# One decoder layer on Trainium2: where copies, additions and weight differences stand among seven block products

## The chip, the cores and the metric

The kernel runs on 1 core of one Trainium2 chip, in fp32 stored data and fp32r matrix products. The metric is the device time of one execution in microseconds (us): median of several executions, smaller is better.

## The reference, cut to what matters

One layer of a decoder with 512 tokens and a model width of 1024. A mixer (retention and dilated attention, gated) gives a 512 x 1024 matrix that is multiplied by `w_o` and added to the residual `x`. Then comes an MLP with 4096 hidden columns, and a gated embedding at the end.

```python
x = x + (gate_r * ret_branch + gate_a * att_branch) @ w_o      # 512x1024 @ 1024x1024
u = rmsnorm(x, g_mlp) @ w_up                                   # 1024 -> 4096
x = x + jnp.square(jax.nn.relu(u)) @ w_down                    # 4096 -> 1024
gate_p = jax.nn.sigmoid(rmsnorm(x, g_ple) @ w_ple_gate)
return x + gate_p * (p_i @ w_ple_proj)
```

The change touches the product with `w_o` and the four products that `w_down` is cut into (each 512 x 1024 by 1024 x 1024). These are the five places where the kernel calls `seven_gemm`.

## The kernel before, in words

**Precision.** Each fp32 factor is split into two parts: hi (rounded to fp32r, by ScalarE, L237) and lo (the difference to the original, by VectorE, L238). A product is three matmuls: hi*hi, hi*lo, lo*hi (`mm3`, L249 to L251), all with 512 columns, into one PSUM bank of 128 x 512.

**Seven products.** `seven_gemm` computes a 2 x 2 block product with seven block products instead of eight. Its left factors (sums and differences of the activation blocks) are prepared by `seven_left`. A product is called here by the number `m` that the code gives it; they run in the order 4, 3, 5 (interleaved), 2, 1, 7, 6. Each has two halves `u` of the contraction and two halves `p` of 128 tokens: 6 matmuls for each pair (u, p), 24 in all. The results lie in PSUM banks: products 4 and 2 share the bank pair named 4 (product 2 accumulates onto 4), 3 and 6 share pair 3, 5 and 7 share pair 5, and product 1 has a pair of its own, `banks[1, p]`. Pairs 3 and 4 show in the trace as `pg`, pairs 5 and 1 as `pb`.

**What is done with a full bank.** ScalarE copies bank pair 4 to the tiles `m4` (L1040, it is needed again after product 1). `acc` (L1026, VectorE) adds a bank with a factor to the residual tiles `x`. When a half of a token tile of `x` is final, `done` calls `ready`, where one is given, which queues a transposition for a few ticks later: `split_T` transposes the 128 x 512 piece on TensorE into a bank (L325), and the result is read twice, hi by ScalarE (L338) and lo by VectorE (L339): `h2h`, `h2l` in the first call, `h3h`, `h3l` in the last. For the tiles that are final after product 5, **the bank that takes the transposes is `banks[1, p]`**, the one into which product 1 is computed next (`free` in `ready`). The three calls between have no `ready` and no transposes.

**Weights.** `plan_seven` lists 14 weight units for each call, numbered 0 to 13 here (n to n + 13 in the code): 0 to 5 for products 4, 3, 5 of both halves, 6 and 7 for product 2, 8 and 9 for product 1, 10 and 11 for product 7, 12 and 13 for product 6. Units 0, 1, 3, 4 and 10 to 13 are sums: one load by SyncE's queue (L200), a second load that adds to it by GpSimd's queue (L202). Units 8 and 9 have no load: they are unit 6 minus unit 2 and unit 7 minus unit 5, subtracted in place by VectorE (L215). `ahead` loads and splits units in order up to `used + n` where `units(n)` adds the class's `AHEAD`: with AHEAD = 3, product number k in order of units splits up to unit k + 3 before its matmuls. There are 6 raw buffers and 4 pairs of split buffers (`whi`, `wlo`), so that the split of a unit waits for the product four units before it.

**Order.** In the first call (with `w_o`) and in the last (last quarter of `w_down`), ScalarE and VectorE execute their instructions strictly in the order of the program text (`manual_schedule`); in the three calls between, and on all other engines and queues, a list scheduler orders the instructions by program order and modelled readiness. In `tail`, AHEAD is 3 when the first and the last call begin; `seven_gemm` sets it to 2 ahead of product 7, so it is 2 when the calls between begin. In `tail`, one tick pops one queued function; a tick comes after each half `p` of a product.

Of the kernel before, what the change touches and what calls it, by code (L numbers as in the profile page):

```python
# [13 lines left out]
AF = mybir.ActivationFunctionType  # L14
ALU = mybir.AluOpType
# [57 lines left out]
def R(ap):  # L73
    return ap.bitcast(F32R)


class Block:
# [86 lines left out]
    def plan_seven(self, w, r0):  # L164


        q = lambda i, j, u: w[r0 + 512 * i + 256 * u : r0 + 512 * i + 256 * (u + 1), 512 * j : 512 * (j + 1)]
        n = len(self.plan)
        for u in range(2):
            self.plan.append(((q(1, 0, u), q(0, 0, u)), None))  # L170
            self.plan.append(((q(0, 1, u), q(1, 1, u)), None))
            self.plan.append((q(1, 1, u), None))
        for u in range(2):
            self.plan.append((q(0, 0, u), None))
        self.differences[n + 7] = [(n + 6 + u, n + 2 + 3 * u) for u in range(2)]
        for u in range(2):
            self.plan.append(((None, n + 6 + u, n + 2 + 3 * u), None))
        for u in range(2):
            self.plan.append(((q(1, 0, u), q(1, 1, u)), None))
        for u in range(2):  # L180
            self.plan.append(((q(0, 0, u), q(0, 1, u)), None))
# [23 lines left out]
    def ahead(self, n):  # L205
        while len(self.loaded) < min(len(self.plan), self.used + n):
            i = len(self.loaded)
            self.fetch(i + 1)
            raw, g0 = self.raws[i]
            src = self.plan[i][0]  # L210
            if isinstance(src, tuple) and src[0] is None:
                g0 = None
            self.loaded.append(self.split_unit(raw, g0))
            for v, w in self.differences.get(i, ()):
                self.nc.vector.tensor_tensor(self.raws[v][0], self.raws[v][0], self.raws[w][0], op=ALU.subtract)  # L215

    def units(self, n):
        self.ahead(n + (0 if self.pinned else self.AHEAD))
# [782 lines left out]
    def seven_gemm(self, U, xs, f, ready):  # L1001


        nc = self.nc
        LEFT = {1: 3, 2: 4, 3: 0, 4: 6, 5: 1, 6: 5, 7: 2}
        banks = {}

        def product(m, bank, u, first, last):
            (wh, wl), = self.units(1)
            for p in range(2):  # L1010
                if first and m != 1:
                    banks[bank, p] = self.gbank() if m in (3, 4) else self.bank("pb")
                ps = banks[bank, p]
                for k in range(2):
                    kk = 2 * u + k
                    c = slice(LEFT[m] * 256 + p * P, LEFT[m] * 256 + (p + 1) * P)
                    sh, sl = (R(U[i][kk].rearrange("p a b -> p (a b)")[:, c]) for i in range(2))
                    self.mm3(ps, sh, sl, wh[:, k], wl[:, k], first and k == 0, last and k == 1, m != bank)
                self.tick()

        X = lambda i, j, p: xs[2 * i + p][:, 512 * j : 512 * (j + 1)]

        def acc(i, j, p, v, sign=0):
            t, x = 2 * i + p, X(i, j, p)
            c = sign * NT + t
            nc.vector.scalar_tensor_tensor(x, v, f[:, c : c + 1], x, op0=ALU.mult, op1=ALU.add)  # L1026

        def done(i, j, p):
            if ready is not None:
                ready(2 * i + p, j, banks.get((1, p)))  # L1030

        for u in range(2):
            for m in (4, 3, 5):
                product(m, m, u, u == 0, u == 1)
        m4 = []
        for p in range(2):
            banks[1, p] = self.bank("pb")
        for p in range(2):
            t = self.tmp("m4")
            nc.scalar.activation(t, banks[4, p], AF.Copy)  # L1040
            m4.append(t)
            acc(0, 1, p, banks[3, p])
            acc(0, 1, p, banks[5, p], 1)
            done(0, 1, p)
        for u in range(2):
            product(2, 4, u, False, u == 1)
        for p in range(2):
            acc(1, 0, p, banks[4, p])
            done(1, 0, p)
            acc(1, 1, p, banks[4, p], 1)  # L1050
        for u in range(2):
            product(1, 1, u, u == 0, u == 1)
        for p in range(2):
            nc.vector.tensor_tensor(m4[p], m4[p], banks[1, p], op=ALU.add)
            acc(0, 0, p, m4[p])
            acc(1, 1, p, m4[p])
        self.AHEAD = 2
        for u in range(2):
            product(7, 5, u, False, u == 1)
        for p in range(2):  # L1060
            acc(0, 0, p, banks[5, p])
            done(0, 0, p)
        for u in range(2):
            product(6, 3, u, False, u == 1)
        for p in range(2):
            acc(1, 1, p, banks[3, p])
            done(1, 1, p)
# [165 lines left out]
```

## Time and profile before

| | us |
|---|---|
| median of 3 runs (993.36 to 993.88) | 993.45 |
| the profiled execution | 993.55 |
| its span, first to last instruction | 991.8 |
| TensorE matmul busy in it | 984.9 |
| VectorE busy | 648.8 |
| ScalarE busy | 462.1 |
| first call of `seven_gemm` on TensorE | 558.15 to about 599.9 |
| last call | 900.15 to about 941.6 |

How to read it: the span is that of the profiled execution; its time also holds some 1.75 us around the span. In rows of the timeline the first number is the start in us from the start of the span, the second the duration, then engine, line, operation, tiles as output<-inputs, and in brackets the idle time of the engine before the row with what ended it. PE is TensorE, DVE VectorE, ACT ScalarE, POOL GpSimd, SPq the queue of SyncE. A matmul is listed with its duration from entry to end, and the next one enters before it ends.

### The profile page before, as it was taken

The numbers are of one execution on the slowest core, as the hardware profiler recorded it, in microseconds if no ns is written. First come the engines' busy times: TensorE is split into PE (matmuls) and PEld (weight loads), VectorE is DVE, ScalarE is ACT, GpSimd is POOL, SyncE is SP. The second block draws the span as 40 slices with busy tenths as digits, with TensorE's granted clock in tenths as the row PEclk, the third lists the DMA queues.
The fourth block names the chain that finished last, engine by engine and source line by source line (L and its number), as shares of the span: only waits on it lengthen the run. The fifth ranks groups of instructions, "written<-read, shape, count | busy, mean of one in ns | idle before, by whom it ended". The sixth has DMA issues, their size and how long they took to land.

```text
span 991.8 us, 12456 instructions
## 1 busy us (share of the span) xinstructions
PE 984.9 (99%) x4588; PEld 826.7 (83%) x4588; DVE 648.8 (65%) x1015; ACT 462.1 (47%) x939; POOL 98.1 (10%) x98
## 2 busy tenths in 40 slices
PE   9999999999999999999999999999999999999998
PEld 6888899889888888888888888888888888888886
DVE  7858675774869345454733796678667769767953
ACT  6635344433334334243423448664563565465451
POOL 0310120220000010001002000100101001000000
PEclk9999999999999999999999999999999999999999
DMA  9723122333234322222446486758749767875911
GB/s 333 262 85 87 44 85 85 113 98 98 83 109 153 124 63 76 96 65 86 162 135 156 137 218 201 185 141 221 184 132 226 187 159 170 228 174 128 298 54 54
DMA packets 90910, 141.16 MB, mean 142 GB/s; under 512 B 6320, under 2 KB 40672, under 8 KB 90848
## 3 DMA queue, kind: packets, MB, share of 16 engines
q1 hardware_dynamic: 79824, 119.36, 37.3%
q0 software_dynamic: 10880, 20.97, 12.6%
q8 instruction: 36, 0.59, 0.2%
q14 instruction: 26, 0.21, 0.1%
q10 hardware_dynamic: 144, 0.02, 0.0%
HBM read 136.10 MB, written 4.24 MB: 141 GB/s over the span
## 4 chain that ended last, share of the span: by engine, by line
PE 97%; DVE 1%; ACT 1%; DMA 1%; SPq 0%; issue 0%; ACTq 0%; DVEq 0%
PE pg L249 27%; PE pg L251 27%; PE pg L250 27%; PE pb L251 3%; PE pb L250 3%; PE pb L249 3%; PE po L699 1%; PE ph L555 1%; PE pt L325 1%; PE sc L676 1%; PE ry L905 1%; PE pe L647 1%; PE kv L893 1%; PE sc L682 1%; PE ry L907 1%; DMA raw<-in_w_in 1%
## 5 line engine op out<-in xcount | busy, mean ns | idle before, releaser
L238 DVE TENSOR_TENSOR wlo<-raw,whi 128x1024 fp32r<-128x1024 f32 (+1 forms) x166 | 196.8, 1190 | 104.3 <-ACT whi L237 102.4
L237 ACT ACTIVATE whi<-raw 128x1024 fp32r<-128x1024 f32 (+1 forms) x165 | 169.7, 1033 | 194.9 <-PE pg L251 71.5
L249 PE MATMUL pg<-whi,hh 128*128 128x512 f32 x440 | 177.3, 403 | 0.0
L251 PE MATMUL pg<-whi,hl 128*128 128x512 f32 x440 | 172.2, 391 | 0.0
L250 PE MATMUL pg<-wlo,hh 128*128 128x512 f32 x440 | 171.9, 391 | 0.0
L251 PEld LDWEIGHTS pg<-whi,hl 128*128 128x128 f32 x440 | 90.4, 206 | 15.1
L249 PEld LDWEIGHTS pg<-whi,hh 128*128 128x128 f32 x440 | 90.5, 206 | 13.8
L250 PEld LDWEIGHTS pg<-wlo,hh 128*128 128x128 f32 x440 | 90.7, 206 | 13.6
L249 PE MATMUL pg<-h2h,whi 128*128 128x512 f32 x256 | 99.6, 389 | 0.0
L250 PE MATMUL pg<-h2l,whi 128*128 128x512 f32 x256 | 99.6, 389 | 0.0
L251 PE MATMUL pg<-h2h,wlo 128*128 128x512 f32 x256 | 99.6, 389 | 0.0
L242 ACT ACTIVATE whi<-raw,gcol 128x256 fp32r<-128x256 f32 (+1 forms) x144 | 66.2, 525 | 22.1 <-PE pg L250 12.4
L243 DVE SCALAR_TENSOR_TENSOR wlo<-raw,gcol,whi 128x256 fp32r<-128x256 f32 (+1 forms) x144 | 65.6, 511 | 15.6 <-ACT whi L242 15.6
L202 POOL DMA_DIRECT2D raw<-in_w_down x32 | 38.6, 1206 | 302.8 <-DMA raw<-in_w_down 188.2
L249 PE MATMUL pg<-hh,whi 128*128 128x512 f32 x160 | 64.0, 400 | 0.0
L249 PE MATMUL pg<-whi,uh 128*128 128x512 f32 x160 | 62.8, 393 | 0.1
L251 PE MATMUL pg<-whi,ul 128*128 128x512 f32 x160 | 62.5, 392 | 0.0
L250 PE MATMUL pg<-wlo,uh 128*128 128x512 f32 x160 | 62.5, 391 | 0.0
L251 PE MATMUL pg<-hh,wlo 128*128 128x512 f32 x160 | 62.4, 390 | 0.0
L250 PE MATMUL pg<-hl,whi 128*128 128x512 f32 x160 | 62.3, 389 | 0.0
L250 PEld LDWEIGHTS pg<-h2l,whi 128*128 128x128 f32 x256 | 48.1, 188 | 10.0
L249 PEld LDWEIGHTS pg<-h2h,whi 128*128 128x128 f32 x256 | 48.1, 188 | 9.9
(201 smaller groups left out, 1693.2 us busy)
## 6 DMA issues: line engine op xcount, KB each, us to landing
raw<-in_w_in SPq DMA_DIRECT2D x72, 512.0 KB, 3.9
raw<-in_w_down SPq DMA_DIRECT2D x48, 512.0 KB, 4.3
raw<-in_w_up SPq DMA_DIRECT2D x32, 512.0 KB, 4.8
raw<-in_w_down POOLq DMA_DIRECT2D x32, 512.0 KB, 6.7
raw<-in_w_o SPq DMA_DIRECT2D x12, 512.0 KB, 3.9
x<-in_x SPq DMA_DIRECT2D x8, 512.0 KB, 6.9
raw<-in_w_ret_out SPq DMA_DIRECT2D x8, 512.0 KB, 3.5
raw<-in_w_o POOLq DMA_DIRECT2D x8, 512.0 KB, 5.8
```

Source lines behind the costliest of these rows:

```text
L202: self.nc.gpsimd.dma_start(raw, rows(add[0]), accum_op=ALU.add)
L237: self.pin(nc.scalar.activation(R(hi[:, i]), raw[:, i], AF.Copy))
L238: nc.vector.tensor_tensor(R(lo[:, i]), raw[:, i], hi[:, i], op=ALU.subtract)
L242: self.pin(nc.scalar.activation(R(hi[:, i]), raw[:, i], AF.Copy, scale=g))
L243: nc.vector.scalar_tensor_tensor(R(lo[:, i]), raw[:, i], g, hi[:, i], op0=ALU.mult, op1=ALU.subtract)
L249: t.matmul(ps, sh, mh, start=first, stop=False, skip_group_check=more)
L250: t.matmul(ps, sh, ml, start=False, stop=False, skip_group_check=more)
L251: t.matmul(ps, sl, mh, start=False, stop=last, skip_group_check=more)
L325: nc.tensor.transpose(ps[:, k * P : (k + 1) * P], part[:, k * P : (k + 1) * P], self.ident)
L555: self.nc.tensor.transpose(ps[:, t * P : (t + 1) * P], rots[t][:, h * HD : (h + 1) * HD], self.ident)
L647: self.nc.tensor.transpose(ps[:, k * P : (k + 1) * P], e[:, k * P : (k + 1) * P], self.ident)
L676: nc.tensor.matmul(sc[:, h * P : (h + 1) * P], qT[:, h, rs], kT[:, h, rs], start=True, stop=True)
```

## The change

The order of the matmuls stays: 4, 3, 5 for u = 0, then 4, 3, 5 for u = 1. What moves is the work of the other engines between them:

- the copies of bank pair 4 now stand right behind product 4, u = 1; the additions of pair 3 right behind product 3, u = 1; the additions of pair 5 stay behind product 5, u = 1;
- AHEAD is 2 for product 5, u = 1, so that unit 8 is not split there, and 3 from the end of the additions of pair 5 on, so that units 8 and 9 are both split ahead of product 2, u = 0 (in every call, also the three between, until it is set to 2 ahead of product 7 as before);
- the two weight differences, until now one behind the other after the split of unit 7, stand each right ahead of the split of its own unit 8 or 9, and so behind the additions of pair 5.

```diff
     def plan_seven(self, w, r0):
...
-        self.differences[n + 7] = [(n + 6 + u, n + 2 + 3 * u) for u in range(2)]
         for u in range(2):
+            self.differences[n + 8 + u] = n + 6 + u, n + 2 + 3 * u
             self.plan.append(((None, n + 6 + u, n + 2 + 3 * u), None))
...
     def ahead(self, n):
...
                 g0 = None
+            if i in self.differences:
+                v, w = (self.raws[k][0] for k in self.differences[i])
+                self.nc.vector.tensor_tensor(v, v, w, op=ALU.subtract)
             self.loaded.append(self.split_unit(raw, g0))
-            for v, w in self.differences.get(i, ()):
-                self.nc.vector.tensor_tensor(self.raws[v][0], self.raws[v][0], self.raws[w][0], op=ALU.subtract)
...
     def seven_gemm(self, U, xs, f, ready):
...
-        for u in range(2):
-            for m in (4, 3, 5):
-                product(m, m, u, u == 0, u == 1)
-        m4 = []
+        for m in (4, 3, 5):
+            product(m, m, 0, True, False)
+        m4 = [self.tmp("m4") for _ in range(2)]
+        product(4, 4, 1, False, True)
+        for p in range(2):
+            nc.scalar.activation(m4[p], banks[4, p], AF.Copy)
+        product(3, 3, 1, False, True)
+        for p in range(2):
+            acc(0, 1, p, banks[3, p])
+        self.AHEAD = 2
+        product(5, 5, 1, False, True)
         for p in range(2):
             banks[1, p] = self.bank("pb")
         for p in range(2):
-            t = self.tmp("m4")
-            nc.scalar.activation(t, banks[4, p], AF.Copy)
-            m4.append(t)
-            acc(0, 1, p, banks[3, p])
             acc(0, 1, p, banks[5, p], 1)
             done(0, 1, p)
+        self.AHEAD = 3
         for u in range(2):
             product(2, 4, u, False, u == 1)
```

## The prediction

> **What bounds the kernel now.** I read the page first, then the chain of waits around the two hand-ordered calls, then the timeline there and in the calls between.
>
> ```profile
> span 991.8 us, 12456 instructions
> PE 984.9 (99%) x4588; PEld 826.7 (83%) x4588; DVE 648.8 (65%) x1015; ACT 462.1 (47%) x939; POOL 98.1 (10%) x98
> PEclk9999999999999999999999999999999999999999
> ```
>
> TensorE is the bound almost everywhere: 984.9 of 991.8 us busy, full clock in all 40 slices. No matmul is removed or reordered by the change, so the question is only which waits of TensorE go and which come. The chain leaves TensorE in two places near the change (start, length, what):
>
> ```profile
> 569.86 1.07 ACT whi L237
> 570.96 1.23 DVE wlo L238
> 572.18 1.14 DVE raw L215
> 573.43 1.06 ACT whi L237
> 574.49 0.49 ACT m L1040
> 575.02 0.50 PE pg L249
> ...
> 918.26 0.76 DVE x L1026
> 919.06 0.66 PE pb L325 x4
> ```
>
> In the first call the split of unit 7, a difference, the split of unit 8 and only then the copy of bank pair 4 release product 2 at 575.02. In the last call a transposition waits for an addition. These chains look long, but how long TensorE itself stood still is a row of the waits over the whole span:
>
> ```profile
> PEld pb L325 <- DVE x L1026: 1.1, 2, 0.8
> PEld pg L249 <- ACT m L1040: 0.7, 2, 0.5
> ```
>
> All that the change can win is in these two rows: 0.7 us for the copies and 1.1 us for the additions, 1.8 us together. Weight loads run ahead of matmuls, so this is an upper bound; in starts of matmuls it is about 1.1 us.
>
> **The change part by part: earlier copies and additions.** They remove no instruction. They free bank pair 4 for product 2, which in the first call can then start one matmul step behind the last matmul of product 5, by the rows below 0.23 us (574.34 to 574.57) and not 0.45 us (574.57 to 575.02). Alone this is worth at most the 1.8 us above. It does not reach the end, because of the next part.
>
> **The change part by part: the differences.** Two subtractions on VectorE move from a place ahead of the additions to a place behind them, interleaved with the splits of units 8 and 9. With AHEAD 2 and then 3, both units stand ahead of product 2 in program order, and the transposes of the tiles of pair 5 are queued only by the ticks of product 2. So in a hand-ordered call the order on VectorE behind the last addition becomes: difference 8, lo of unit 8, difference 9, lo of unit 9, then the two `h2l` reads of the transposed bank. Before, only lo of unit 9 stood there, its hi being long ready. The rows, first call and then last:
>
> ```profile
> 572.10 2.35 DVE L215 TENSOR_TENSOR raw<-raw,raw 128x1024 f32<-128x1024 f32 x2
> 573.43 1.06 ACT L237 ACTIVATE whi<-raw 128x1024 fp32r<-128x1024 f32 x1 [2.51 <-DVE raw L215]
> 574.52 1.23 DVE L238 TENSOR_TENSOR wlo<-raw,whi 128x1024 fp32r<-128x1024 f32 x1
> 574.34 0.39 PE L250 MATMUL pb<-wlo,uh 128*128 128x512 f32 x1
> 574.57 0.39 PE L251 MATMUL pb<-whi,ul 128*128 128x512 f32 x1
> 575.02 0.50 PE L249 MATMUL pg<-whi,uh 128*128 128x512 f32 x1
> 578.03 0.75 DVE L1026 SCALAR_TENSOR_TENSOR x<-pb,one,x 128x512 f32<-128x512 f32 x1
> 578.70 1.22 DVE L238 TENSOR_TENSOR wlo<-raw,whi 128x1024 fp32r<-128x1024 f32 x1
> 579.83 1.28 DVE L339 TENSOR_TENSOR h2l<-pb,h2h 128x512 fp32r<-128x512 f32 x2
> 581.19 1.23 DVE L238 TENSOR_TENSOR wlo<-raw,whi 128x1024 fp32r<-128x1024 f32 x1
> 581.72 0.39 PE L249 MATMUL pb<-whi,uh 128*128 128x512 f32 x1
> ...
> 916.24 0.39 PE L251 MATMUL pb<-whi,ul 128*128 128x512 f32 x1
> 921.57 1.28 DVE L339 TENSOR_TENSOR h3l<-pb,h3h 128x512 fp32r<-128x512 f32 x2
> 923.44 0.39 PE L249 MATMUL pb<-whi,uh 128*128 128x512 f32 x1
> ```
>
> The decisive dependency: the transposes lie in `banks[1, p]`, and product 1 (`pb`, 581.72 and 923.44) overwrites this bank, so it cannot start before `h2l` has read it. Before, the two reads ended at 579.83 + 1.28 = 581.11, some 0.6 us ahead of product 1: hidden. Now the chain. From a start to the next start, by these rows: difference to hi of the same unit 573.43 - 572.10 = 1.33; hi to lo 574.52 - 573.43 = 1.09; lo to the next VectorE instruction 579.83 - 578.70 = 1.13; addition to the next 578.70 - 578.03 = 0.67; one `h2l` read 1.28 / 2, about 0.68 to its end. The last addition starts when product 5 has filled its bank, as this row pair shows for VectorE reading a fresh bank: entry of the last matmul to start of the addition 600.29 - 599.67 = 0.62.
>
> ```profile
> 599.67 0.39 PE L251 MATMUL pg<-whi,ul 128*128 128x512 f32 x1
> 600.29 1.41 DVE L1026 SCALAR_TENSOR_TENSOR x<-pg,one,x 128x512 f32<-128x512 f32 x2
> ```
>
> First call: last addition at 574.57 + 0.62 = 575.19, difference 8 at 575.86, then 1.33 + 1.09 + 1.13 (difference 9 at 579.41), 1.33 + 1.09 + 1.13 (first `h2l` at 582.96), read until 583.64, product 1 a little later (0.05): 583.7, against 581.72. That is +2.0 us. Last call: 916.24 + 0.62 + 0.67 + 7.10 + 0.68 + 0.05 = 925.36 against 923.44: +1.9 us. The early start of product 2 is swallowed, since product 1 is now released by VectorE and not by product 2; nothing is to be subtracted for it. The second read ends 0.6 us after the first, within the six matmuls of p = 0 (6 x 0.23 us), so it adds nothing. The sum of this part, +3.9 us, reaches the end whole, since TensorE is the chain. VectorE idles twice for a hi in it (1.1 us each); the earlier additions win nothing here, because the last one hangs on product 5 alone.
>
> **What is late next.** Lo of unit 10, behind the two reads, moves from 581.19 to about 584.3, 3.1 us, while TensorE moves by 2.0. The next tight place (of the first row, a stretch of the windows: length, then busy us of PE, PEld, DVE, ACT, POOL):
>
> ```profile
> 582.00:598.00 16.00, 16.00 (x80) 13.31 (x79) 15.93 (x21) 6.35 (x9) 0.00 (x0) 1.00 0.75 203
> 594.80 1.41 DVE L1026 SCALAR_TENSOR_TENSOR x<-pb,one,x 128x512 f32<-128x512 f32 x2
> 596.04 0.60 PE L325 MATMUL pt<-ident,x 128*128 128x128 f32 x4
> ```
>
> VectorE has no gaps there in which to catch up, 15.93 of 16 us being busy. The first of these additions ends at 594.80 + 0.75 = 595.55, 0.5 us ahead of its transposes. VectorE being 1.1 us further behind, TensorE waits up to 0.6 us there, or nothing if the scheduler places the transposes some matmuls later. I take the middle, 0.3 in each hand-ordered call: +0.6 in all, with 0 and 1.3 as ends.
>
> **Raw buffers and queues.** The differences also free the raw buffers of units 2 and 5, for the loads of units 12 and 13:
>
> ```profile
> 573.34 1.56 SPq L200 DMA_DIRECT2D raw<-in_w_o  x2
> 580.08 1.22 POOL L202 DMA_DIRECT2D raw<-in_w_o  x1 [1.58 <-DMA raw<-in_w_ple_proj]
> 588.65 1.06 ACT L237 ACTIVATE whi<-raw 128x1024 fp32r<-128x1024 f32 x1 [0.91 <-DMA raw<-in_w_o]
> 593.67 1.22 DVE L238 TENSOR_TENSOR wlo<-raw,whi 128x1024 fp32r<-128x1024 f32 x1
> ```
>
> The second of the two loads was issued by 574.9; now it waits for difference 9 (end about 580.6), some 6 us later, and behind it on SyncE's queue stand all later loads, behind its adding load on GpSimd's queue nothing of this call. The hi of unit 13 moves from 588.65 to about 594.7; its lo, due in VectorE's stream at 593.67 + 3.1 = 596.8, has 0.9 us left over. Price 0, with an end of +1.5 us per call if a transfer is slower by 2.5 us, behind the loads that now overlap it.
>
> **The three calls between.** There the scheduler already does what the change writes down: in the second of them the first copy (746.55) follows the product at once, ahead of the differences.
>
> ```profile
> 746.55 0.60 ACT L1040 ACTIVATE m<-pg 128x512 f32<-128x512 f32 x1 [0.30 <-PE pg L251]
> 768.71 1.06 ACT L237 ACTIVATE whi<-raw 128x1024 fp32r<-128x1024 f32 x1 [2.60 <-DMA raw<-in_w_down]
> 771.12 1.22 DVE L238 TENSOR_TENSOR wlo<-raw,whi 128x1024 fp32r<-128x1024 f32 x1
> 772.41 0.48 PE L250 MATMUL pg<-wlo,uh 128*128 128x512 f32 x1
> ```
>
> There are no transposes in bank 1, so no new wait. The lower rank of the second difference could delay it by one to three additions (0.7 to 2.0 us), and with it the load of unit 13. In this call unit 13 is just in time (lo ends at 772.34, needed at 772.41), but its lo waited behind VectorE's additions and not for its hi (ends 769.77), so the first 1.3 us of a delay cost nothing. AHEAD 3 only ranks splits earlier. Price 0, ends -0.1 and +0.9.
>
> **The sum.** 2.0 + 1.9 + 0.6 + 0 = +4.5 us on the profiled execution's 993.55, so 998.05 for such an execution; the median of the runs is 0.1 lower, so 993.45 + 4.5 = 997.9, or 0.45% slower.
>
> **The rivals.** (a) The new wait does not come and the old ones go: faster by up to 1.8 us, 991.7, more likely 992.3. It decides where `h2l` of the first tile ends before about 581.1, 2.5 us earlier than I work out, as it would if VectorE could read the bank while difference 9 waits. Against it: at 570.96 lo of unit 7 waits for its hi and the difference behind it, ready by then, does not pass. So VectorE runs in order. (b) The wait comes, but small: the scheduler finds TensorE other work, or steps are shorter; half the sum, 993.2 to 996. Against it: no other product has its weights split at that time. (c) The wait comes and brings more: late loads of unit 13 (up to 1.5 us per call), 0.9 between, or the clock. A stop of TensorE of some 2.5 us stands nowhere inside this trace, where the clock is full in all slices; were it halved for as long as the stop, 2.5 us of matmuls would lose 1.2 us per call. All together 999.5 to 1003. [...]
>
> **How the numbers follow.** A measurement of this kernel tells about 0.2% (2 us) from no change: the borders are 991.46 and 995.44. Forecast (996 to 999.5): 0.70. (c) 0.12. (a) 0.10, of which 0.03 beyond the border of faster. (b) 0.08, of which 0.06 below 995.44. Faster 0.03, same 0.07 + 0.06 = 0.13, slower 0.84. The range leaves out (a), part of (b) and the upper half of (c): 995.0 to 1000.6.
>
> **What would show it.** In the changed profile: the wait of the weight load of product 2 for the copy (L1040) gone in both calls; a new wait of about 2 us, weight load or matmul of `pb` L249 for `h2l` and `h3l` L339, 9 us behind the last matmul of product 5; the order difference, lo, difference, lo, `h2l` on VectorE. Were product 1 not waiting for L339, the argument is wrong; were the rows between different by more than 1 us, my price of 0 there is.

## The result, and the profile after

The changed kernel takes 999.28 us (median of six runs, 998.51 to 1000.64) against 993.45 us for the kernel before (six runs, 993.16 to 993.98): ratio 1.0059, 95% interval 1.0046 to 1.0072, 5.8 us slower. The forecast was 997.9 in 995.0 to 1000.6. The profiled execution took 998.93 us.

In the changed kernel, the lines behind L215 are numbered one higher: matmuls L250 to L252, split hi L238 and lo L239, additions L1027, transposes L326, reads of the transposed bank L339 and L340, differences still L215. First the page, the span and the busy times:

```profile
span 997.1 us, 12446 instructions
PE 986.5 (99%) x4588; PEld 828.3 (83%) x4588; DVE 648.1 (65%) x1015; ACT 461.3 (46%) x939; POOL 98.0 (10%) x98
```

The span is 5.3 us longer (997.1 - 991.8) with the same 4588 matmuls. TensorE is busy 1.6 us more (986.5 - 984.9) and stands still 3.7 us more (10.6 against 6.9). So two things happened: it waited, and for a while it ran slower. The waits over the whole span show the first:

```profile
PEld pb L250 <- DVE h2l L340: 2.6, 1, 2.6
PEld pb L250 <- DVE h3l L340: 2.6, 1, 2.6
PE pb L250 <- DVE h2l L340: 2.2, 1, 2.2
PE pb L250 <- DVE h3l L340: 2.2, 1, 2.2
```

One wait in each hand-ordered call, of the first matmul of product 1 for the VectorE read of the transposed bank. The old row of product 2 waiting for the copy of bank pair 4 is gone. How the new wait comes about stands in the chain that ended last, around the first stop (start, length, what):

```profile
574.76 0.75 DVE x L1027
575.51 1.15 DVE raw L215
576.71 0.04 issue
576.76 1.07 ACT whi L238
577.85 1.23 DVE wlo L239
579.08 1.15 DVE raw L215
580.33 1.07 ACT whi L238
581.42 1.01 DVE wlo L239
582.43 0.14 issue
582.56 0.69 DVE h2l L340
583.30 0.75 PE pb L250
```

The last addition, difference 8, hi, lo, difference 9, hi, lo, read, product 1: TensorE is absent from the chain for 8.5 us (574.76 to 583.30). The timeline of TensorE and VectorE around it, and at the stop of the last call:

```profile
574.33 0.39 PE L252 MATMUL pb<-whi,ul 128*128 128x512 f32 x1
574.56 0.39 PE L250 MATMUL pg<-whi,uh 128*128 128x512 f32 x1
...
575.43 1.22 DVE L215 TENSOR_TENSOR raw<-raw,raw 128x1024 f32<-128x1024 f32 x1
577.85 1.23 DVE L239 TENSOR_TENSOR wlo<-raw,whi 128x1024 fp32r<-128x1024 f32 x1 [1.21 <-ACT whi L238]
579.00 1.22 DVE L215 TENSOR_TENSOR raw<-raw,raw 128x1024 f32<-128x1024 f32 x1
...
580.71 0.39 PE L252 MATMUL pg<-whi,ul 128*128 128x512 f32 x1
581.42 1.23 DVE L239 TENSOR_TENSOR wlo<-raw,whi 128x1024 fp32r<-128x1024 f32 x1 [1.21 <-ACT whi L238]
582.56 1.28 DVE L340 TENSOR_TENSOR h2l<-pb,h2h 128x512 fp32r<-128x512 f32 x2
583.30 0.75 PE L250 MATMUL pb<-whi,uh 128*128 128x512 f32 x1 [2.20 <-DVE h2l L340]
...
925.83 0.39 PE L252 MATMUL pg<-whi,ul 128*128 128x512 f32 x1
928.41 0.50 PE L250 MATMUL pb<-whi,uh 128*128 128x512 f32 x1 [2.19 <-DVE h3l L340]
```

Product 2 does start early: at 574.56, one step of 0.23 us behind the last matmul of product 5. It only reaches its end earlier (580.71) and waits there. The second effect is in the windows (length; busy us of PE, PEld, DVE, ACT, POOL; granted clock; DMA share; GB/s): the first stop, the time behind it, then the same for the last call.

```profile
580.00:583.30 3.30, 1.10 (x5) 0.56 (x4) 2.09 (x4) 2.97 (x5) 1.21 (x2) 1.00 0.83 254
583.30:587.00 3.70, 3.70 (x9) 2.97 (x10) 3.70 (x6) 1.90 (x3) 1.22 (x1) 0.54 0.86 166
925.80:928.40 2.60, 0.42 (x2) 0.00 (x0) 1.87 (x3) 2.60 (x5) 1.22 (x2) 1.00 0.81 214
928.40:932.00 3.60, 3.59 (x16) 2.92 (x17) 3.60 (x6) 0.97 (x2) 1.13 (x1) 1.00 0.97 219
```

Behind the first stop the granted clock is 0.54: 9 matmuls in 3.7 us, where the last call runs 16 in 3.6 us. The clock record of this trace (the times at which the granted clock changes) puts this half-clock stretch at 583.38, 3.41 us long. Behind the equal stop of the last call there is none. The page's row of 40 slices, all nines, hides it, a slice being 25 us.

The balance, from starts of the same matmuls in both traces (after minus before):

| place | shift | what |
|---|---|---|
| last matmul of product 5, first call | -0.2 | 574.33 - 574.57; so from the start of the call, ahead of all that is changed |
| first matmul of product 2, first call | -0.5 | 574.56 - 575.02; the copies' gain is 0.2 |
| first matmul of product 1, first call | +1.6 | 583.30 - 581.72; 1.8 from the end of product 5 |
| end of the first call | +3.3 | the half-clock stretch, 1.7; the shift is 3.3 from its end (586.79) on |
| end of the three calls between | +3.2 | they cost nothing |
| first matmul of product 1, last call | +5.0 | 928.41 - 923.44; 1.8 from the start of this call |
| end | +5.3 | 0.1 behind product 1, 0.2 at the transposes of product 6 |

So in this execution the two stops cost 3.6 us and the half-clock stretch 1.7; the loads that now come late cost TensorE nothing in the first call.

### The profile page after: what moved, and what is told of

It is laid out like the page before. It is cut to its first block, busy times and chain, and to the rows that moved or that the text cites. A ratio compares the mean times of both kernels' runs of the same rounds, so it can differ in the third digit from the quotient of the medians.

```text
span 997.1 us, 12446 instructions
## 1 busy us (share of the span) xinstructions
PE 986.5 (99%) x4588; PEld 828.3 (83%) x4588; DVE 648.1 (65%) x1015; ACT 461.3 (46%) x939; POOL 98.0 (10%) x98
## 4 chain that ended last, share of the span: by engine, by line
PE 98%; DVE 1%; ACT 0%; issue 0%; ACTq 0%
PE pg L250 27%; PE pg L252 27%; PE pg L251 26%; PE pb L250 3%; PE pb L251 3%; PE pb L252 3%; PE po L700 1%; PE ph L556 1%; PE pt L326 1%; PE sc L677 1%; PE ry L906 1%; PE pe L648 1%; PE kv L894 1%; PE sc L683 1%; PE ry L908 1%; DVE raw L215 0%
## 5 line engine op out<-in xcount | busy, mean ns | idle before, releaser
L239 DVE TENSOR_TENSOR wlo<-raw,whi 128x1024 fp32r<-128x1024 f32 (+1 forms) x166 | 196.6, 1190 | 108.5 <-ACT whi L238 106.8
L238 ACT ACTIVATE whi<-raw 128x1024 fp32r<-128x1024 f32 (+1 forms) x165 | 169.1, 1031 | 201.8 <-PE pg L252 59.1
L250 PE MATMUL pg<-whi,hh 128*128 128x512 f32 x440 | 177.2, 403 | 0.0
L252 PE MATMUL pg<-whi,hl 128*128 128x512 f32 x440 | 172.2, 391 | 0.0
L252 PEld LDWEIGHTS pg<-whi,hl 128*128 128x128 f32 x440 | 90.4, 205 | 15.0
L250 PEld LDWEIGHTS pg<-whi,hh 128*128 128x128 f32 x440 | 90.5, 206 | 13.8
L250 PE MATMUL pg<-h2h,whi 128*128 128x512 f32 x256 | 99.6, 389 | 0.0
L252 PE MATMUL pg<-h2h,wlo 128*128 128x512 f32 x256 | 99.6, 389 | 0.0
L250 PE MATMUL pg<-hh,whi 128*128 128x512 f32 x160 | 64.0, 400 | 0.0
L250 PE MATMUL pg<-whi,uh 128*128 128x512 f32 x160 | 62.7, 392 | 0.0
L252 PE MATMUL pg<-hh,wlo 128*128 128x512 f32 x160 | 62.4, 390 | 0.0
L252 PE MATMUL pg<-whi,ul 128*128 128x512 f32 x160 | 62.3, 391 | 0.0
L252 PEld LDWEIGHTS pg<-h2h,wlo 128*128 128x128 f32 x256 | 48.0, 188 | 10.1
```

Source lines behind the costliest of these rows:

```text
L238: self.pin(nc.scalar.activation(R(hi[:, i]), raw[:, i], AF.Copy))
L239: nc.vector.tensor_tensor(R(lo[:, i]), raw[:, i], hi[:, i], op=ALU.subtract)
L250: t.matmul(ps, sh, mh, start=first, stop=False, skip_group_check=more)
L252: t.matmul(ps, sl, mh, start=False, stop=last, skip_group_check=more)
```

## The experiments

Two theories were tested against each other. A: the change costs what TensorE waits for the VectorE chain of differences, splits and reads. B: in addition, a stop of about 2 us or more (an estimate from the 2.20 us of the changed kernel's first stop) brings the half clock, which is worth some 1.5 us each time. Rivals were the loads of units 12 and 13, now late, and that stops of this length leave the clock full. The kernel before ran in the same jobs: 993.34 us beside the first four, 993.45 beside the three stops, 993.36 beside the last three. Medians:

| run | us | ratio (95% interval) | wait of product 1 in each call |
|---|---|---|---|
| changed kernel | 999.28 | 1.0059 (1.0046 to 1.0072) | 2.2, 2.2 |
| unit 9 split later | 995.48 | 1.0023 (1.0013 to 1.0033) | none; 1.3 in product 6 |
| differences back | 992.21 | 0.9989 (0.998 to 0.9998) | none |
| differences alone | 995.69 | 1.0025 (1.0015 to 1.0034) | 1.1, 1.1 |
| differences spread | 992.28 | 0.9992 (0.9983 to 1.0002) | none |
| spread, AHEAD as before | 992.19 | 0.9988 (0.9979 to 0.9996) | none |
| change without AHEAD | 996.26 | 1.0028 (1.0017 to 1.0038) | 1.6, 1.4 |
| one load for units 12, 13 | 997.89 | 1.0052 (1.0038 to 1.0065) | 2.2, 2.2 |
| before, 2 splits more | 995.01 | 1.0014 (1.0005 to 1.0023) | 0.8, 0.7 |
| before, 3 splits more | 1000.55 | 1.0065 (1.0053 to 1.0078) | 2.0, 2.0 |
| before, 4 splits more | 1002.33 | 1.0087 (1.0073 to 1.0101) | 3.3, 3.3 |

**Differences back.** The changed kernel with both differences behind the split of unit 7, as before the change:

```diff
+        self.differences[n + 7] = [(n + 6 + u, n + 2 + 3 * u) for u in range(2)]
...
-            self.differences[n + 8 + u] = n + 6 + u, n + 2 + 3 * u
...
-            if i in self.differences:
-                v, w = (self.raws[k][0] for k in self.differences[i])
-                self.nc.vector.tensor_tensor(v, v, w, op=ALU.subtract)
             self.loaded.append(self.split_unit(raw, g0))
+            for v, w in self.differences.get(i, ()):
+                self.nc.vector.tensor_tensor(self.raws[v][0], self.raws[v][0], self.raws[w][0], op=ALU.subtract)
```

> The change without its difference part: both differences stand behind the split of unit 7 again, while copies and additions are early and AHEAD is 2, then 3 as in the change. Theory A: the hi parts of units 8 and 9 are then ready early, so that two additions, two lo and the two reads follow each other without idle time; reads end near 580.8, about when product 1 can start; no stop, and the waits for the copies are gone too: 992.0 to 993.3. Rival 2 (the early copies and additions, or AHEAD, are what costs): 996.5 to 999.5, as after the change.

Measured: 992.21 us, 1.1 us faster than before. Its VectorE timeline (lines as before the change):

```profile
572.22 2.35 DVE L215 TENSOR_TENSOR raw<-raw,raw 128x1024 f32<-128x1024 f32 x2
574.49 1.40 DVE L1026 SCALAR_TENSOR_TENSOR x<-pg,one,x 128x512 f32<-128x512 f32 x2
575.81 1.40 DVE L1026 SCALAR_TENSOR_TENSOR x<-pb,one,x 128x512 f32<-128x512 f32 x2
577.13 2.35 DVE L238 TENSOR_TENSOR wlo<-raw,whi 128x1024 fp32r<-128x1024 f32 x2
579.39 1.28 DVE L339 TENSOR_TENSOR h2l<-pb,h2h 128x512 fp32r<-128x512 f32 x2
```

The same instructions without a bracket, so without idle time: the hi parts are made while VectorE adds. The reads start at 579.39 instead of 582.56, and product 1 waits for nothing. So the early copies and additions are worth 1.1 us, what the prediction had as their worth in starts of matmuls. The loss comes with the moved differences; what the AHEAD part adds to it is shown below.

**Differences alone.** The kernel before with only the differences moved:

```diff
-        self.differences[n + 7] = [(n + 6 + u, n + 2 + 3 * u) for u in range(2)]
         for u in range(2):
+            self.differences[n + 8 + u] = n + 6 + u, n + 2 + 3 * u
...
+            if i in self.differences:
+                v, w = (self.raws[k][0] for k in self.differences[i])
+                self.nc.vector.tensor_tensor(v, v, w, op=ALU.subtract)
             self.loaded.append(self.split_unit(raw, g0))
-            for v, w in self.differences.get(i, ()):
-                self.nc.vector.tensor_tensor(self.raws[v][0], self.raws[v][0], self.raws[w][0], op=ALU.subtract)
```

> The kernel before, with the differences alone moved, each right ahead of the split of its own unit. Theory A: difference 9 and a hi that is no longer ready stand between the last addition and the reads, so the reads come 2.4 us later and product 1 stops for about 1.3 us per call, the waits for the copies stay: 995.5 to 997, without half clock where the stop is this short. Rival 2: no change, 993.0 to 994.0.

Measured: 995.69, full clock in all nine runs (mean over the span 0.999 or more). Product 1 waits, but half as long as in the whole change:

```profile
PE pb L250 <- DVE h2l L340: 1.1, 1, 1.1
PE pb L250 <- DVE h3l L340: 1.1, 1, 1.1
```

Moving the differences is a loss by itself, 2.35 us. These two parts do not add up to the change: -1.1 and +2.35 would make +1.2, the change makes +5.8.

**Change without AHEAD.** The same change, with AHEAD left as before (the line `self.AHEAD = 2` ahead of product 5 and `self.AHEAD = 3` behind its additions deleted):

```diff
-        self.AHEAD = 2
         product(5, 5, 1, False, True)
...
-        self.AHEAD = 3
```

> The change without its AHEAD part (AHEAD stays 3, or 2 in the calls between, as before): difference 8 and lo of unit 8 then stand between the additions of pair 3 and those of pair 5, and only difference 9 and lo of unit 9 between the last addition and the reads. Theory A: reads end about 1 us earlier than after the change, stop of 1.2 to 1.7 us per call, short enough for a full clock: 995.0 to 996.8. Rival (AHEAD is without effect): 998.5 to 1000.

Measured: 996.26, full clock in all seven runs. Here difference 8 and its split stand ahead of the additions of pair 5 and not behind them, and one of the two idle times of VectorE falls where it delays less:

```profile
574.04 1.22 DVE L215 TENSOR_TENSOR raw<-raw,raw 128x1024 f32<-128x1024 f32 x1
576.47 1.23 DVE L239 TENSOR_TENSOR wlo<-raw,whi 128x1024 fp32r<-128x1024 f32 x1 [1.21 <-ACT whi L238]
577.61 1.41 DVE L1027 SCALAR_TENSOR_TENSOR x<-pb,one,x 128x512 f32<-128x512 f32 x2
```

The AHEAD part lengthens the stops from 1.6 and 1.4 to 2.2 each, 1.4 us together. It costs 3.0 us (999.28 - 996.26); the other 1.6 is about one half-clock stretch, which this kernel has in no run.

**Unit 9 split later.** The changed kernel, but AHEAD is set to 3 only behind u = 0 of product 2, so that difference 9 and its split stand behind the reads:

```diff
-        self.AHEAD = 3
         for u in range(2):
             product(2, 4, u, False, u == 1)
+            self.AHEAD = 3
```

> The change, but AHEAD stays 2 for product 2, u = 0, so that on VectorE only difference 8 and lo of unit 8 stand between the last addition and the reads of bank 1 (h2l, h3l); difference 9 and lo of unit 9 follow them. Theory A (product 1 waits for these reads, since they stand behind both differences and splits in VectorE's order): the reads move 3.5 us earlier, end near 580.3 in the first call, the stop of 2.2 us ahead of product 1 goes and with it the half clock; unit 9 is then late for the second half of product 1 by at most 0.5 us per call. Time 992.5 to 994.0. Rival 1 (the loss is the late weights of units 8 and 9 and late loads of 12 and 13, not the reads): unit 9 comes even later, so the time stays or grows: 998.5 to 1001.

Measured: 995.48, 1.5 us over the upper end of theory A's range. The direction is right: the stop ahead of product 1 is gone. But a new one has come in product 6, in both calls; first the row of the waits, with both of them in it,

```profile
PE pg L251 <- DVE wlo L239: 2.5, 2, 1.3
```

then the timeline of the first call:

```profile
582.76 2.36 DVE L239 TENSOR_TENSOR wlo<-raw,whi 128x1024 fp32r<-128x1024 f32 x2 [1.19 <-ACT whi L238]
...
596.37 1.22 DVE L239 TENSOR_TENSOR wlo<-raw,whi 128x1024 fp32r<-128x1024 f32 x1
597.64 0.50 PE L251 MATMUL pg<-wlo,uh 128*128 128x512 f32 x1 [1.26 <-DVE wlo L239]
```

VectorE still idles 1.2 us for each hi, and behind 582.76 it has no gap to catch up in, so that lo of unit 13 comes 1.3 us late for product 6. The idle time was moved, not removed. My expectation had followed only the first place that it reached. One of the eight runs, the longest (996.45), has a mean clock of 0.998, as a run with one half-clock stretch has; the others have 0.999 or more. No trace of that run is kept.

**Differences spread, and the same with AHEAD as before.** In the changed kernel, difference 8 stands behind the split of unit 6 and difference 9 behind that of unit 7 (`ahead` subtracts behind the split, as in the kernel before); the second kernel also deletes the two AHEAD lines.

```diff
-            self.differences[n + 8 + u] = n + 6 + u, n + 2 + 3 * u
+            self.differences[n + 6 + u] = [(n + 6 + u, n + 2 + 3 * u)]
```

> The change, but difference 8 stands behind the split of unit 6 and difference 9 behind the split of unit 7, ahead of the additions. Theory A: difference 8 fills 1.2 us in which VectorE idles ahead of lo of unit 7, the reads end 1.2 us earlier than with both behind unit 7 (near 579.6), product 1 is never stopped and the waits for the copies are gone: 991.8 to 993.0. Rival 1: raw buffers are freed earlier still, so 991.5 to 992.5; rival 2: 996.5 to 999.5.

> The version with difference 8 behind unit 6 and difference 9 behind unit 7 and the early copies and additions, but with AHEAD left as in the kernel before. Theory A: unit 8 is then split ahead of the additions of pair 5, with hi ready early and no idle time of VectorE; the reads end no later than in the version with AHEAD 2: 991.8 to 993.0, the same as that version (992.28) within 0.4. Rival 2 (AHEAD 2 behind product 5 is what gives the gain): 993.2 to 994.

Measured: 992.28 and 992.19, the same as with both behind unit 7. Difference 8 fills a time in which VectorE waited for a hi anyway, and the reads come 1 us earlier (spread kernel's VectorE):

```profile
569.64 1.22 DVE L216 TENSOR_TENSOR raw<-raw,raw 128x1024 f32<-128x1024 f32 x1
...
578.43 1.28 DVE L340 TENSOR_TENSOR h2l<-pb,h2h 128x512 fp32r<-128x512 f32 x2
```

That gains nothing more, since nothing waits for them any longer; nor is the AHEAD part needed. These three versions have medians some 1.1 us (0.1%) below the kernel before; the interval of the spread one reaches to 1.0002, so for it alone a gain is not shown.

**Stops made to measure.** The kernel before, with lo of unit 9 computed two, three or four times more in the first and the last call (the same values again). Nothing moves but VectorE's time ahead of the reads, 1.26 us for each (first call: lo of unit 9 to the first read 1.13 us before, 3.65 us with two more, 4.91 us with three):

```diff
+        if w is self.w_o or r0 == 3072:
+            self.again.add(n + 9)
...
-                nc.vector.tensor_tensor(R(lo[:, i]), raw[:, i], hi[:, i], op=ALU.subtract)
+                for _ in range(1 + (3 if len(self.loaded) in self.again else 0)):
+                    nc.vector.tensor_tensor(R(lo[:, i]), raw[:, i], hi[:, i], op=ALU.subtract)
```

> The kernel before; in the first and the last call the lo part of unit 9 is computed three times in place of once (the same values again), ahead of the reads of bank 1. This makes a stop of TensorE ahead of product 1 of 2 x 1.13 us less the 0.6 us that were left over, and less what the wait of product 1 for its last matmul hides: about 1.1 to 1.6 us per call. [...] Rival (VectorE's order is not what stops product 1): 993.2 to 993.8.

> The same with lo of unit 9 four times: stop about 2.2 to 2.7 us per call, as in the changed kernel. Theory B: 997.8 to 998.9 from the stops and 1.5 us for each half-clock stretch, about one per run: 998.5 to 1001, varying by run. [...]

> The same with lo of unit 9 five times: stop about 3.3 to 3.8 us per call. Theory B: two half-clock stretches in nearly every run: 1000.0 to 1001.2 from the stops plus 3 us, 1002.5 to 1004.5. [...]

Measured: 995.01, 1000.55, 1002.33. The step from two to three repeats is 5.5 us where two stops grew by 1.2 us each, 2.4 us together; the other 3.1 is the clock. The window of 10 us with the first stop in it, with two repeats,

```profile
580.00:590.00 10.00, 9.23 (x45) 7.29 (x44) 9.93 (x13) 4.79 (x7) 1.22 (x1) 1.00 0.89 212
```

with three,

```profile
580.00:590.00 10.00, 7.97 (x30) 6.07 (x29) 9.90 (x13) 3.34 (x4) 1.22 (x1) 0.83 0.91 209
```

and with four:

```profile
580.00:590.00 10.00, 6.71 (x23) 5.07 (x23) 9.90 (x11) 2.78 (x3) 0.84 (x1) 0.84 0.88 199
```

With two repeats the clock is 1.00 (in all eleven runs 0.999 or more over the span), and the time is 0.6 below what two stops of the 1.1 us expected at the least would make (993.45 + 2.2): the scheduler has placed two matmuls of product 7 ahead of product 1, which shortens the stop (waits of 0.8 and 0.7 us). With three it is 0.83. The wait is then 2.0 us, 2.4 from start to start of the matmuls around it, and still the trace has a half-clock stretch in both calls: the clock is 0.83 over 580 to 590 and 0.84 over 925 to 936, and in the first call the matmuls from 586.04 to 589.03 follow each other by 0.43 us, where it is 0.23 at full clock. The mean clocks of the five runs (0.996, 0.996, 0.998, 0.996, 0.998) fit two stretches, two, one, two, one; the times go with them, 1000.55 to 1001.14 and 998.96 to 999.26, so that a stretch is worth some 1.5 us. The stops alone, at full clock, gave 997.8 to 998.9; all five runs lie above it, so that the rival of a full clock falls. Four repeats, with stops of 3.7 us from start to start, came 0.2 below theory B's range: of the four runs one (1000.65, clock 0.999) shows no stretch, the others (0.995 to 0.998) do.

**Late loads.** The changed kernel without the second, adding load of units 12 and 13, so that their values are other weights than the reference's; all instructions of the other engines stay.

```diff
-            self.plan.append(((q(0, 0, u), q(0, 1, u)), None))
+            self.plan.append((q(0, 0, u), None))
```

> The changed kernel without the second (adding) load of units 12 and 13, so that product 6 uses other weights and the output is not the reference's: these units are then in place some 5 us earlier. Theory A: the time is set by the stop ahead of product 1, and late loads cost at most what they add behind it: 997.5 to 999.3, stop of 2.2 us in both calls still there. Rival 1 (the loss is mostly late raw loads of units 12 and 13): 993.5 to 995.5.

Measured: 997.89, 1.4 us under the changed kernel, and the two stops of 2.2 us unchanged. So the late loads are not what makes the change slow, though they may cost up to 1.4 us of it. With them out of the way the clock sorts the runs: none at half clock (mean 1.0), 996.97; clock 0.998, 997.89, 997.89 and 998.14; clock 0.996, 1000.43. The run without is 3.6 us over before, the two stops alone. In the changed kernel a full-clock run (998.86) is no faster than those beside it. A fitting reason is that a half-clock stretch also gives the late unit 12 time:

```profile
591.09 1.06 ACT L238 ACTIVATE whi<-raw 128x1024 fp32r<-128x1024 f32 x1 [1.42 <-DMA raw<-in_w_o]
592.18 1.23 DVE L239 TENSOR_TENSOR wlo<-raw,whi 128x1024 fp32r<-128x1024 f32 x1 [1.70 <-ACT whi L238]
```

In the first call of the profiled execution of the changed kernel, ScalarE waits 1.42 us for that load and VectorE 1.70 us for ScalarE, and TensorE waits for neither. Without the half-clock stretch it might reach TensorE. The last call of the same trace is at full clock, and there the same two waits (0.98 and 0.80 us) do not reach TensorE. No profile of a run of the changed kernel at full clock in both calls exists, so this stays argued and not shown.

## Why the prediction was right, and where its terms were off

**The new wait** was the forecast, and it came with its order. Difference, lo, difference, lo, read, each step within 0.1 us of the sum's: read at 582.56 against 582.96 worked out, the last addition at 574.76 against 575.19. Both are 0.4 early because the call starts 0.25 us earlier in this trace and VectorE could read the bank 0.43 us behind the last matmul's entry, not 0.62. The two stops were priced +2.0 and +1.9; they moved product 1 by 1.8 and 1.8. The undoing of the differences (992.21) and the run without half clock (996.97) show both sides of this term.

**The early start of product 2 swallowed** was right: it starts 0.2 us earlier, and the end knows nothing of it. With the differences back it shows as the 1.1 us that the prediction gave it in starts of matmuls.

**The transposes behind**, +0.6 with ends 0 and 1.3, were 0.2: no shift there in the first call, 0.2 in the last.

**The three calls between**, price 0, moved by -0.1. That fits the prediction's reading, that the scheduler already did there what the change writes down.

**The loads of unit 13**, price 0, cost TensorE nothing in the first call of the profiled execution. Unit 12, named there but not worked out, is late too. Between the medians up to 1.4 us hang on the second loads of both units; five and six runs with differing numbers of half-clock stretches cannot tell how much of that is theirs.

**The clock** is the step that was wrong, though it stood among the rivals. The sum had it at nothing and rival (c), which holds it, at 0.12. It fell in five of the six runs of the changed kernel (mean clock 0.996 to 0.998), once or twice. The working, 1.2 us for each stop from half clock as long as the stop, fell short of the measured 1.5 to 1.7, because the stretch is longer (3.41 us against the 2.5 taken). The prediction had no stop of this length in its trace from which to read the term, so that the nothing in its sum was an estimate, which no run shows. In the runs TensorE stood for 2.0 to 2.2 us by the waits, 2.4 to 2.6 from start to start, and the clock fell: to 0.54 over 583.30 to 587.00 in the changed kernel. The forecast of 997.9 is thus 1.4 us under the median: terms of about -0.3 (stops), -0.4 (transposes), and +2 from clock and loads together. That the median still lies within the central forecast, 0.2 us below its upper end, is in part luck: two terms that were too large made up for part of the one that was missing.

**The rivals.** (a), the old waits gone and no new one, is what the kernel becomes with the differences left where they were: 992.2, against 992.3 worked out. (b) did not come about: the differences alone cost about half the sum (2.35 us), but not for its reasons. There difference 8 and its split stand ahead of the additions, so that one unit and not two holds up the reads.

## What to carry to other kernels

Where two engines run in strict order and hand a unit back and forth (difference, hi, lo), leave another instruction's work between the steps: placed back to back, each unit idled VectorE 1.2 us, and in a stream without gaps this idle time came back at the next tight place when one unit was shifted. Before work is moved behind an addition, look at what reads the same bank next and who overwrites it. And do not price a stop of TensorE at its length alone: stops of 2.0 us and more brought some 1.5 us more in most of these runs.

## What the runs showed of the hardware that was not expected

In the changed kernel's trace a stop of TensorE of 2.20 us was followed by a half-clock stretch of 3.41 us (583.38 to 586.79), longer than the stop itself. Waits of 0.7 to 1.6 us ahead of product 1 were followed by none in 27 runs (differences alone, change without AHEAD, two repeats; mean clock 0.999 or more in each). By the mean clocks, waits of 2.0 to 2.2 us were followed by one in most runs, at one or at both of the two stops, in some runs at neither, and the longest stops, 3.7 us from start to start, escaped in one run (1000.65 us, clock 0.999). The granted clock around or behind the stops in the traces:

| kernel | wait in each call, us | clock, first call | clock, last call |
|---|---|---|---|
| changed kernel | 2.20, 2.19 | 0.54 (583.30 to 587.00) | 1.00 (928.40 to 932.00) |
| one load for units 12, 13 | 2.2, 2.2 | 1.0 (mean over the span) | 1.0 (the same) |
| before, 3 splits more | 2.0, 2.0 | 0.83 (580 to 590) | 0.84 (925 to 936) |
| before, 4 splits more | 3.3, 3.3 | 0.84 (580 to 590) | 0.84 (925 to 936) |
| before, 2 splits more | 0.8, 0.7 | 1.00 (580 to 590) | 1.00 (925 to 936) |
| differences alone | 1.1, 1.1 | 1.00 (580 to 590) | 1.00 (925 to 936) |
| change without AHEAD | 1.6, 1.4 | 1.00 (580 to 590) | 1.00 (925 to 936) |

The length of the wait does not tell the two stops of the changed kernel apart. Nor does the time that TensorE was busy in the 3.41 us ahead: 1.21 us ahead of 583.38, where the clock fell, and 1.22 us ahead of 928.41, where it stayed full. What decides between them these runs do not show. Nor is the run at clock 0.998 of the kernel with unit 9 split later explained: the trace of that kernel, from another run, has waits of 1.3 us.
